# One block of tokens through gathered expert rows, the other three densely, in an expert layer that computes all 16384 experts

## The chip, the core and the metric

The kernel runs on one core of a Trainium2 chip. The metric is the device time of one execution in microseconds (us). The engines of a core run side by side, each through its own queue in order: TensorE (PE in the profile; its weight loads are PEld), VectorE (DVE), ScalarE (ACT), GpSimd (POOL) and SyncE (SP), which issues the transfers (DMA) of the kernel before.

## What is computed

Two transformer blocks in float32 over 512 tokens of width 1024. The first block has two mixing branches and then an expert layer; the second has two layers with a context of 256 tokens and ordinary feed-forward parts. The change lies in the expert layer. There are 128 x 128 = 16384 experts, an input row `peer_u` and an output row `peer_v` of 1024 numbers for each. A token has 8 heads; each head takes the best 16 sums of a first and a second key, so a token has 128 chosen experts with gates:

```python
experts = (i1 * PEER_NKEYS + i2).reshape(t, PEER_HEADS * PEER_TOPK)
gates = jax.nn.softmax(cv, axis=-1).reshape(t, PEER_HEADS * PEER_TOPK)

def token_block(args):
    xb, eb, gb = args
    act = jax.nn.gelu(jnp.einsum('tkd,td->tk', expert_u[eb], xb, preferred_element_type=jnp.float32))
    return jnp.einsum('tk,tkd->td', act * gb, expert_v[eb].astype(jnp.float32)).astype(xb.dtype)
```

The result is added to the residual x, and a norm follows.

## The kernel before

Activations are kept feature-major: x is [128, 8, 512], feature within a tile of 128 on partitions, then the tile, then the token. A product of float32 accuracy is three matmuls in float32r, on a high and a low part of each operand (`mm3`, lines 197 to 199). `wload` brings a block of weights (512 KB), lets ACT copy the high part (line 139, called from there) and DVE subtract the low part (`wl`, line 192).

The expert layer (`peer`) computes every expert for every token, without any gather, in these stages:

- norm and scores: `first_blocks` makes the normed x in two parts (`xh`, `xl`); 16 products with `wq` and the sub-keys give the scores `sc`.
- select (`peer_select`): for each of four tiles of 128 tokens DVE finds the best 16 of each key, the best 16 sums, and their indices; at the end come the gates. The indices and gates are transposed into `iT` (tiles `pi`).
- H (`peer_h`): for each second key j, 24 matmuls over 512 tokens (8 feature tiles times three) give 128 experts' activations, ACT applies gelu, and SP writes them to DRAM (`Hd`). It runs as the filler of the select stage and goes on beside G.
- G (`peer_g`): for each token the two one-hot matrices `oa` and `ob` (DVE, lines 898 and 899), one float32 matmul of them (line 901, two records each) and, for four tokens, one ACT copy to `gs`; SP writes these gates of all experts to DRAM (`Gd`).
- V (`peer_v`): for each j the weights V[j], the activations `pa` and the gates `pg` are loaded, DVE multiplies, ACT and DVE split the product into `ph` and `pl`. Five j form a group; for each of the 8 feature tiles a group takes 15 matmuls into a bank of PSUM, and DVE adds the bank to x.

Then the second block begins with its context part (`ctx0`), beside which `x_entry` norms x.

The order in which instructions are issued is made by `interleave` (line 44): generators ("lanes") yield an assumed time on TensorE and a time until their next piece may start; earlier lanes go first when they are ready, and the filler takes the rest. A half of one j of H counts 2.6 there, a piece of select 0 with a pause of 1.6 to 3.0. PSUM has eight banks: five of tag `bk` (`bank`), two `ac` (`accb`), one `po` (`pob`).

Of the kernel before, what the change touches and what calls it, by code (L numbers as in the profile page):

```python
# [102 lines left out]
class Net:  # L103
# [152 lines left out]
    def rstd(s, pool, T):  # L256
        """1 / rms of every token, from the running sum, on all partitions."""
# [35 lines left out]
    def first_blocks(s, pool, xpool, x, gain, shift, r, aside=None):  # L293
# [1507 lines left out]
```

## Time and profile before

| | us |
|---|---|
| median of 3 runs (lowest to highest) | 4282.54 (4280.67 to 4285.31) |
| the profiled execution, span | 4279.0 |
| busy PE, PEld, DVE, ACT, POOL within the span | 4206.2, 3497.0, 2457.2, 1607.1, 3.5 |
| bytes moved by DMA | 532.83 MB |

The profiled execution has no time of its own beside its span; the median lies 3.5 us above that span. Busy times of PE overlap, since matmuls are pipelined: a matmul's own duration is longer than the step from one start to the next, and it is the step that counts for a stage.

### The profile page before, as it was taken

How to read it: one execution, taken by the hardware profiler on the slowest of the kernel's cores; microseconds unless marked ns; L12 is line 12 of the kernel's file. 1: busy time of each engine (PE TensorE's matmuls, PEld its weight loads, DVE VectorE, ACT ScalarE, POOL GpSimd, SP SyncE). 2: the span in 40 equal slices, each digit the busy share in tenths (PEclk: the TensorE clock that was granted, in tenths of full speed). 3: DMA queues.
4: the chain of work that ended last, by engine and by line, in shares of the span. 5: the costliest groups of instructions: out<-in, count | busy, mean ns of one | idle time of the engine just before them, and what ended most of it. 6: DMA issues, size and time to landing. Idle time of an engine off the chain costs nothing.

```text
span 4279.0 us, 59173 instructions
## 1 busy us (share of the span) xinstructions
PE 4206.2 (98%) x22964; PEld 3497.0 (82%) x22964; DVE 2457.2 (57%) x5635; ACT 1607.1 (38%) x2801; POOL 3.5 (0%) x28
## 2 busy tenths in 40 slices
PE   8999999999999999999999999999999999999998
PEld 5878888887788888888888777888888888887887
DVE  7536554699556665766666665665222256665334
ACT  5335454332233333322222464554211244553222
POOL 0000000000000000000000000000000000000000
PEclk9999999999999999999999999999999999999999
DMA  5341133234445455765666454122112122122232
GB/s 194 106 146 66 45 104 114 78 128 134 152 158 185 168 189 193 240 194 191 191 196 197 170 210 137 35 77 72 60 64 65 62 99 87 45 68 91 94 95 83
DMA packets 219544, 532.83 MB, mean 125 GB/s; under 512 B 24064, under 2 KB 82816, under 8 KB 214784
## 3 DMA queue, kind: packets, MB, share of 16 engines
q1 hardware_dynamic: 219264, 529.06, 37.2%
q8 instruction: 181, 2.97, 0.3%
q14 instruction: 99, 0.81, 0.1%
HBM read 455.58 MB, written 73.40 MB: 124 GB/s over the span
## 4 chain that ended last, share of the span: by engine, by line
PE 88%; DVE 8%; ACT 1%; DMA 1%; issue 1%; SPq 0%; DVEq 0%; ACTq 0%
PE ac L197 21%; PE ac L199 21%; PE ac L198 21%; PE po L401 3%; PE bk L198 3%; PE bk L197 3%; PE bk L199 3%; PE bk L901 3%; PE bk L229 3%; DVE wl L192 1%; PE bk L1017 1%; PE bk L552 1%; PE bk L546 1%; DVE peq L142 1%; DVE psi L814 1%
## 5 line engine op out<-in xcount | busy, mean ns | idle before, releaser
L197 PE MATMUL ac<-xh,wh 128*128 128x512 f32 (+1 forms) x3608 | 1359.3, 378 | 16.0 <-ACT xh L139 7.3
L199 PE MATMUL ac<-xh,wl 128*128 128x512 f32 (+1 forms) x3608 | 1338.7, 372 | 6.1 <-DVE wl L192 5.7
L198 PE MATMUL ac<-xl,wh 128*128 128x512 f32 (+1 forms) x3608 | 1337.8, 372 | 0.9 <-DVE xl L145 0.7
L139 ACT ACTIVATE wh<-wr 128x1024 fp32r<-128x1024 f32 (+1 forms) x599 | 629.5, 1053 | 1723.3 <-PE ac L198 1602.2
L192 DVE TENSOR_TENSOR wl<-wr,wh 128x1024 fp32r<-128x1024 f32 (+1 forms) x599 | 726.5, 1214 | 608.8 <-ACT wh L139 584.7
L197 PEld LDWEIGHTS ac<-xh,wh 128*128 128x128 f32 x3608 | 681.3, 189 | 152.5 <-issue 18.5
L199 PEld LDWEIGHTS ac<-xh,wl 128*128 128x128 f32 x3608 | 680.9, 189 | 137.0 <-DVE wl L192 13.4
L198 PEld LDWEIGHTS ac<-xl,wh 128*128 128x128 f32 x3608 | 681.8, 189 | 121.3 <-issue 7.8
L898 DVE TENSOR_SCALAR oa<-iota,pi 128x128 f32<-128x128 f32 x512 | 144.1, 282 | 148.2 <-PE bk L901 148.2
L197 PE MATMUL bk<-ph,wh 128*128 128x512 f32 x512 | 199.5, 390 | 1.2 <-ACT ph L139 1.2
L198 PE MATMUL bk<-pl,wh 128*128 128x512 f32 x512 | 199.5, 390 | 0.4 <-DVE pl L142 0.4
L199 PE MATMUL bk<-ph,wl 128*128 128x512 f32 x512 | 199.3, 389 | 0.0
L198 PE MATMUL ac<-pl,wh 128*128 128x512 f32 x512 | 199.2, 389 | 0.0
L199 PE MATMUL ac<-ph,wl 128*128 128x512 f32 x512 | 199.2, 389 | 0.0
L197 PE MATMUL ac<-ph,wh 128*128 128x512 f32 x512 | 199.2, 389 | 0.0
L142 DVE TENSOR_TENSOR pa<-pa,pg 128x512 f32<-128x512 f32 x128 | 87.8, 689 | 180.8 <-DMA pg<-Gd 131.0
L198 PE MATMUL ac<-al,wh 128*128 128x512 f32 (+1 forms) x528 | 186.8, 354 | 0.0
L199 PE MATMUL ac<-ah,wl 128*128 128x512 f32 (+1 forms) x528 | 186.8, 354 | 0.0
L197 PE MATMUL ac<-ah,wh 128*128 128x512 f32 (+1 forms) x528 | 186.7, 354 | 0.0
L899 DVE TENSOR_SCALAR ob<-iota,pi,pi 128x128 f32<-128x128 f32 x512 | 174.5, 341 | 0.0
L145 DVE SCALAR_TENSOR_TENSOR x<-ac,mod,x 128x512 f32<-128x512 f32 (+1 forms) x64 | 46.3, 725 | 191.3 <-PE ac L199 191.0
L901 PEld LDWEIGHTS bk<-ob,oa 128*128 128x128 f32 x1024 | 135.1, 191 | 11.3 <-ACT wh L139 0.4
(407 smaller groups left out, 5522.5 us busy)
## 6 DMA issues: line engine op xcount, KB each, us to landing
wr<-win SPq DMA_DIRECT2D x151, 512.0 KB, 3.5
wr<-U SPq DMA_DIRECT2D x128, 512.0 KB, 3.7
wr<-V SPq DMA_DIRECT2D x128, 512.0 KB, 4.6
mw<-wmod SPq DMA_DIRECT2D x96, 512.0 KB, 4.2
Hd<-h SPq DMA_DIRECT2D x128, 256.0 KB, 2.3
pa<-Hd SPq DMA_DIRECT2D x128, 256.0 KB, 4.3
Gd<-gs SPq DMA_DIRECT2D x32, 1024.0 KB, 5.5
pg<-Gd SPq DMA_DIRECT2D x25, 1280.0 KB, 7.9
```

The source lines that it names most:

```text
L139: s.nc.scalar.activation(out, in_, AF.Copy, **kw)
L142: s.nc.vector.tensor_tensor(out, a, b, op=op)
L145: s.nc.vector.scalar_tensor_tensor(out, a, sc, b, op0=op0, op1=op1)
L192: (eng or nc.vector).tensor_tensor(lo[:, :nk, :], raw[:, :nk, :], r32(hi[:, :nk, :]), op=ALU.subtract)
L197: mm(out, ah, bh, start=start, stop=False)
L198: mm(out, ah, bl, start=False, stop=False)
L199: mm(out, al, bh, start=False, stop=stop)
L229: s.nc.tensor.transpose(out, in_, s.ident)
L401: s.nc.tensor.matmul(po, vs[j], pt[:, j, :], start=j == 0, stop=j == nb - 1, skip_group_check=True)
L898: nc.vector.tensor_scalar(a1, iota, iT[0][:, tok:tok + 1], None, op0=ALU.is_equal)
L899: nc.vector.tensor_scalar(a2, iota, iT[1][:, tok:tok + 1], iT[2][:, tok:tok + 1], op0=ALU.is_equal, op1=ALU.mult)
L901: nc.tensor.matmul(b[:, i * 128:(i + 1) * 128], a1, a2, start=True, stop=True)
```

## The change

It leaves the mixing branches and the second block as they are, and does this in the expert layer (TS = 128 tokens, TD = 384):

- The first 128 tokens leave the dense path. Once their choices are known (`rows`, the number of the expert row), `sparse_u` gathers for each of the 128 choices the 128 tokens' rows of `peer_u` (a second copy of that input, laid out in rows, `Ur`): one indirect DMA from GpSimd brings [128 tokens, 1024], 512 KB, into one of six buffers, and DVE multiplies it with the normed x of these tokens (`xt`, token-major, from eight transposes in `first_blocks`) and sums, in one `tensor_tensor_reduce`. Gathers are issued four ahead. Gelu and gates follow.
- `sparse_v` gathers for each of these tokens the 128 rows of `peer_v` (512 KB), four tokens at a time, and sums them with float32 matmuls of 32 columns, one token's weights in one column of a window of zeros, into two banks. Eleven of its 32 steps stand beside G, the rest in V.
- H, G and V handle 384 tokens: the matmuls of H have 384 columns, `Hd` is written for two j at a time, G makes 96 groups of four tokens rather than 128.
- In G the one-hot `oa` is no longer made by DVE: POOL subtracts for four tokens at once, ACT applies Abs and then Relu(1 - a).
- V is turned: the activations are the stationary operand (128 tokens) and V[j] is streamed in two halves of 512 columns; the sums over all 128 j stay in six PSUM banks (three tiles of tokens, two halves), so the adds into x after each group go. At the end eight copies bring the banks to SBUF, 32 transposes and eight adds bring them into x.
- x waits in DRAM (`keep`, 2 MB) from the norm to the end, because four of the six gather buffers lie in its room; SP loads it back when the gathered sums are through.
- The assumed times in the generators change (2.1 for half a j of H, 1.5 rather than 1.7 for G, 4.1 for a j of V).

Comments and docstrings also go; that changes nothing. The diff, cut to its core:

```diff
+TS = 128
+TD = SEQ - TS
...
+                if each:
+                    each(k, t, sl)
...
+                if tt:
+                    s.transpose(b[:, c * 128:(c + 1) * 128], ix)
+                    nc.vector.tensor_copy(iT[c][:, (tt - 1) * 128:tt * 128], b[:, c * 128:(c + 1) * 128])
+            if tt == 0:
+                e = s.t(p, "ppf", [128, 128], 1)
+                s.stt(e, ixs[1], 128.0, ixs[0], ALU.mult, ALU.add)
+                nc.vector.tensor_copy(S["rows"], e)
+                s.transpose(b[:, 0:128], e)
+                nc.vector.tensor_copy(S["rowsT"], b[:, 0:128])
+                S["chosen"] = True
...
+    def gather(s, S, table, idx):
+        g = S["ring"][S["n"] % len(S["ring"])]
+        S["n"] += 1
+        s.nc.gpsimd.indirect_dma_start(out=g, out_offset=None, in_=table,
+                                       in_offset=bass.IndirectOffsetOnAxis(ap=idx, axis=0))
+        return g
+    def sparse_u(s, S):
+        nc = s.nc
+        yield lambda: "chosen" in S
+        act = S["act"]
+        ahead = []
+        for k in range(128 + 4):
+            if k < 128:
+                ahead.append(s.gather(S, s.I["Ur"], S["rows"][:, k:k + 1]))
+            if k >= 4:
+                g = ahead.pop(0)
+                nc.vector.tensor_tensor_reduce(g, g, S["xt"], scale=1.0, scalar=0.0, op0=ALU.mult, op1=ALU.add,
+                                               accum_out=act[:, k - 4:k - 3])
+                yield 0.0, 1.7
+        yield lambda: "gated" in S
+        s.act(act, act, AF.Gelu_apprx_tanh)
+        s.tt(act, act, flat(S["ge"]), ALU.mult)
+        b = s.bank()
+        s.transpose(b[:, 0:128], act)
+        nc.vector.tensor_copy(S["aT"], b[:, 0:128])
+        S["weighted"] = True
+    def sparse_v(s, S):
+        nc = s.nc
+        yield lambda: "weighted" in S
+        rows = s.I["V"].rearrange("j p a b -> (j p) (a b)")
+        po = S["po"] = [s.pob(), s.bank()]
+        aT = S["aT"].rearrange("p (g t) -> p t g", t=32)
+        for t in range(32):
+            gs = [s.gather(S, rows, S["rowsT"][:, 32 * g + t:32 * g + t + 1]) for g in range(4)]
+            w = S["w"][t % len(S["w"])]
+            nc.vector.tensor_copy(w[:, :, 31], aT[:, t, :])
+            for h in range(2):
+                for g in range(4):
+                    nc.tensor.matmul(po[h][32 * g:32 * g + 32, :], w[:, g, 31 - t:63 - t],
+                                     gs[g][:, 512 * h:512 * h + 512], start=t == 0, stop=t == 31,
+                                     skip_group_check=True)
+            yield 2.0, 12.0
+        S["summed"] = True
...
+            ps = s.accb()[:, :TD]
             for k in range(8):
-                s.mm3(ps, w[0][:, k, :], w[1][:, k, :], xh[:, k, :], xl[:, k, :], k == 0, k == 7)
+                s.mm3(ps, w[0][:, k, :], w[1][:, k, :], xh[:, k, TS:], xl[:, k, TS:], k == 0, k == 7)
                 if k == 3:
-                    yield 2.6, 0.0
-            h = s.t(hp, "h", [128, SEQ], 2)
-            s.act(h, ps, AF.Gelu_apprx_tanh)
-            s.nc.sync.dma_start(Hd[j], h)
-            yield 2.6, 0.0
+                    yield 2.1, 0.0
+            if j % 2 == 0:
+                h = s.t(hp, "h", [128, 2, TD], 2)
+            s.act(h[:, j % 2], ps, AF.Gelu_apprx_tanh)
+            if j % 2:
+                s.nc.sync.dma_start(Hd[j // 2], h)
+            yield 2.1, 0.0
...
+        for tb in range(TD // 32):
             gs = s.t(gp, "gs", [128, 128, 32], 2)
             for i4 in range(8):
                 b = s.bank()
+                t0 = tb * 32 + i4 * 4
+                a1 = s.t(gp, "oa", [128, 4, 128], 2)
+                nc.gpsimd.tensor_tensor(a1, iota[:, None, :].to_broadcast([128, 4, 128]),
+                                        iT[0][:, t0:t0 + 4, None].to_broadcast([128, 4, 128]), op=ALU.subtract)
+                nc.scalar.activation(a1, a1, AF.Abs)
+                nc.scalar.activation(a1, a1, AF.Relu, scale=-1.0, bias=1.0)
                 for i in range(4):
-                    tok = tb * 32 + i4 * 4 + i
-                    a1, a2 = s.t(gp, "oa", [128, 128], 4), s.t(gp, "ob", [128, 128], 4)
-                    nc.vector.tensor_scalar(a1, iota, iT[0][:, tok:tok + 1], None, op0=ALU.is_equal)
+                    tok = t0 + i
+                    a2 = s.t(gp, "ob", [128, 128], 4)
                     nc.vector.tensor_scalar(a2, iota, iT[1][:, tok:tok + 1], iT[2][:, tok:tok + 1],
                                             op0=ALU.is_equal, op1=ALU.mult)
-                    nc.tensor.matmul(b[:, i * 128:(i + 1) * 128], a1, a2, start=True, stop=True)
+                    nc.tensor.matmul(b[:, i * 128:(i + 1) * 128], a1[:, i], a2, start=True, stop=True)
                 s.copy(gs[:, :, i4 * 4:i4 * 4 + 4], b.rearrange("p (t i) -> p i t", t=4))
-                yield 0.9, 1.7
+                yield 0.9, 1.5
...
+            Hd = dp.tile([64, 128, 2, TD], F32, name="Hd")
+            Gd = dp.tile([TD // 32, 128, 128, 32], F32, name="Gd")
+            keep = dp.tile([128, 8, SEQ], F32, name="keepx")
...
+                     ring=[flat(x[:, 2 * n:2 * n + 2, :]) for n in range(4)]
+                     + [s.t(sp, f"sr{n}", [128, DM], 1) for n in range(2)])
...
+            su, sv = s.sparse_u(S), s.sparse_v(S)
+            interleave([s.peer_select(p, sc, iota, iT, S), su], hs)
         with ExitStack() as t:
             gp = s.pool(t, "gb")
             s.mark("H+G")
-            interleave([s.peer_g(gp, iota, iT, Gd)], hs)
+            interleave([s.peer_g(gp, iota, iT, Gd), s.until(sv, 12)], hs)
...
+        acc = [[s.accb() if t == 0 else s.bank() for _ in range(2)] for t in range(3)]
+        def dense():
+            js = 0
+            for E in [2] + [6] * 21:
+                g = s.t(p0 if js == 0 else p1, "pg", [128, TD // 32, E, 32], 1 if js == 0 else 2)
+                nc.sync.dma_start(g, Gd[:, :, js:js + E, :].rearrange("b p j t -> p b j t"))
+                for e in range(E):
+                    p, n = (p0, 2) if js % 4 < 2 else (p1, 2)
+                    vh, vl = s.wload(s.I["V"][js], 8, p, n)
+                    if js % 2 == 0:
+                        a = s.t(p0 if js == 0 else p1, "pa", [128, 2, TD], 1 if js == 0 else 2)
+                        nc.sync.dma_start(a, Hd[js // 2])
+                    av = a[:, js % 2].rearrange("p (b t) -> p b t", t=32)
+                    s.tt(av, av, g[:, :, e, :], ALU.mult)
+                    ah, al = s.t(p, "ph", [128, TD], n, F32R), s.t(p, "pl", [128, TD], n, F32R)
+                    s.split(ah, al, a[:, js % 2])
+                    vh, vl = flat(vh), flat(vl)
+                    for h in range(2):
+                        hh = slice(512 * h, 512 * h + 512)
+                        for t in range(3):
+                            tt = slice(128 * t, 128 * t + 128)
+                            s.mm3(acc[t][h], ah[:, tt], al[:, tt], vh[:, hh], vl[:, hh], js == 0, js == 127)
+                    js += 1
+                    yield 4.1, 0.0
+            assert js == 128
+        def reload():
+            yield lambda: "summed" in S
+            for k in range(8):
+                nc.sync.dma_start(x[:, k, :], keep[:, k, :])
+        interleave([sv, reload(), dense()])
+        y = s.t(p1, "py", [128, 4, DM], 1)
+        for h in range(2):
+            hh = slice(512 * h, 512 * h + 512)
+            s.copy(y[:, 0, hh], S["po"][h])
+            for t in range(3):
+                (s.copy if t % 2 else nc.vector.tensor_copy)(y[:, t + 1, hh], acc[t][h])
+        for m in range(8):
+            b = s.bank()
+            for t in range(4):
+                s.transpose(b[:, t * 128:(t + 1) * 128], y[:, t, m * 128:(m + 1) * 128])
+            s.tt(x[:, m, :], x[:, m, :], b, ALU.add)
+            s.squares(p1, x[:, m, :], SEQ)
...
+    A["Ur"] = np.ascontiguousarray(g["peer_u"][0].reshape(128, 128, DM).transpose(1, 0, 2)).reshape(16384, DM)
```

## Rows read from the trace of the kernel before

**Rows 1.** The page: the span and the busy time of each engine.

```profile
span 4279.0 us, 59173 instructions
PE 4206.2 (98%) x22964; PEld 3497.0 (82%) x22964; DVE 2457.2 (57%) x5635; ACT 1607.1 (38%) x2801; POOL 3.5 (0%) x28
```

**Rows 2.** Busy time by stretch: length, then PE, PEld, DVE, ACT, POOL with instruction counts, granted clock, DMA share, GB/s. Select beside H; H beside G; V; the start of the second block.

```profile
885.00:1110.00 225.00, 221.94 (x958) 177.89 (x957) 221.15 (x766) 62.49 (x81) 0.00 (x0) 1.00 0.45 139
1110.00:1697.00 587.00, 587.00 (x3082) 499.90 (x3081) 358.81 (x1151) 209.21 (x310) 0.00 (x0) 1.00 0.49 175
1697.00:2390.00 693.00, 691.39 (x3045) 570.93 (x3044) 433.68 (x584) 210.06 (x261) 0.00 (x0) 1.00 0.62 197
2390.00:2600.00 210.00, 198.85 (x1591) 158.04 (x1591) 143.29 (x361) 114.63 (x267) 0.00 (x0) 0.98 0.59 210
```

**Rows 3.** Timeline of PE where V begins and where it ends: start, duration, instruction; in brackets idle time and what ended it.

```profile
1710.61 0.39 PE L199 MATMUL ac<-xh,wl 128*128 128x512 f32 x1
1710.84 0.39 PE L197 MATMUL bk<-ph,wh 128*128 128x512 f32 x1
...
2410.01 0.39 PE L199 MATMUL ac<-ph,wl 128*128 128x512 f32 x1
2412.62 1.71 PE L260 MATMUL bk<-na,ones 128*128 128x512 f32 x2 [2.23 <-DVE na L142]
```

**Rows 4.** Timeline of PE around 770 us: matmuls of 256 columns before and after a gap.

```profile
768.00 0.28 PE L198 MATMUL bk<-ml,wh 128*128 128x256 f32 x1
768.12 0.28 PE L199 MATMUL bk<-mh,wl 128*128 128x256 f32 x1
...
774.19 0.79 PE L197 MATMUL ac<-xh,wh 128*128 128x256 f32 x2 [3.31 <-ACT xh L139]
...
775.03 0.41 PE L199 MATMUL ac<-xh,wl 128*128 128x256 f32 x1
775.24 0.41 PE L197 MATMUL ac<-xh,wh 128*128 128x256 f32 x1
```

**Rows 5.** Groups of instructions in the stretch 1110 to 1697 us (H beside G): busy us and mean ns of one, idle before and its releaser.

```profile
L899 DVE TENSOR_SCALAR ob<-iota,pi,pi 128x128 f32<-128x128 f32 x512 | 174.5, 341 | 0.0
...
L901 PE MATMUL bk<-ob,oa 128*128 128x128 f32 x1024 | 136.1, 275 | 0.0
...
L192 DVE TENSOR_TENSOR wl<-wr,wh 128x1024 fp32r<-128x1024 f32 x86 | 104.9, 1219 | 64.3 <-ACT wh L139 64.3
L139 ACT ACTIVATE wh<-wr 128x1024 fp32r<-128x1024 f32 x86 | 91.0, 1059 | 201.4 <-PE ac L198 201.4
L139 ACT ACTIVATE gs<-bk 128x512 f32<-128x512 f32 x128 | 76.0, 594 | 177.8 <-PE bk L901 177.8
L133 ACT ACTIVATE h<-ac 128x512 f32<-128x512 f32 x86 | 49.9, 581 | 0.0
```

**Rows 6.** The same stretch 885 to 1110 us as in Rows 2, for line 192 alone: its DVE time and count, clock, DMA.

```profile
885.00:1110.00 225.00, 47.14 (x39) 1.00 0.45 139
```

**Rows 7.** Line 377, the kernel's `tensor_tensor_reduce`, over the whole run: ns min/median/max of one, by form; its read of the sum is a record of its own.

```profile
L377 DVE DVE_READ_ACCUMULATOR2_ANT sv<- x248: 74/83/86, 234.9 to 3841.4; 128x1 f32 x124
L377 DVE CUSTOM_DVE_ANT_0 apr<-bk,b x16: 678/691/693, 234.2 to 575.7; 128x512 f32<-128x512 f32 x16
```

**Rows 8.** Timeline of PE with float32 matmuls of 32 columns in four places of the array (line 1017, 256 columns, four matmuls in eight records): sixteen records and the start of what follows.

```profile
64.05 0.40 PE L198 MATMUL ac<-xl,wh 128*128 128x512 f32 x1
...
72.23 1.07 PE L1017 MATMUL bk<-mw,modl 128*32 128x256 f32 x16
73.24 0.50 PE L197 MATMUL ac<-xh,wh 128*128 128x512 f32 x1
```

**Rows 9.** DMA issues: KB of one, median us from issue to landing; then for V[j] the least, median and longest landing.

```profile
wr<-U SPq DMA_DIRECT2D x128, 512.0 KB, 3.7
wr<-V SPq DMA_DIRECT2D x128, 512.0 KB, 4.6
...
pg<-Gd SPq DMA_DIRECT2D x1, 768.0 KB, 8.2
...
DMA to landing us min/median/max: 3.4/4.6/7.6
```

**Rows 10.** Timeline of SP and of DVE from the last gates to the first product of V.

```profile
1675.95 0.80 SPq L905 DMA_DIRECT2D Gd<-gs  x2
...
1680.18 0.84 SPq L187 DMA_DIRECT2D wr<-U  x1
1681.12 0.83 SPq L975 DMA_DIRECT2D pg<-Gd  x1
...
1691.12 1.28 DVE L142 TENSOR_TENSOR pa<-pa,pg 128x512 f32<-128x512 f32 x2
```

**Rows 11.** Timeline of DVE at the end of V and the start of the second block.

```profile
2410.43 0.69 DVE L142 TENSOR_TENSOR x<-x,ac 128x512 f32<-128x512 f32 x1 [1.26 <-PE ac L199]
2411.88 0.69 DVE L142 TENSOR_TENSOR na<-na,nsq 128x512 f32<-128x512 f32 x1 [0.76 <-ACT nsq L253]
2412.60 0.88 DVE L145 SCALAR_TENSOR_TENSOR nt<-cx,mod,nr 128x256 f32<-128x256 f32 x2
```

**Rows 12.** Busy time of one 50 us stretch at the start of V, columns as in Rows 2.

```profile
1700.00:1750.00 50.00, 48.56 (x211) 38.88 (x210) 34.16 (x42) 22.42 (x26) 0.00 (x0) 1.00 0.78 257
```

More of the change, by code (lines that the diff above doesn't have):

```diff
@@ L291, in last_blocks, with first_blocks @@
         return r
-    def first_blocks(s, pool, xpool, x, gain, shift, r, aside=None):
+    def first_blocks(s, pool, xpool, x, gain, shift, r, aside=None, each=None):
         s.prime(2)
@@ L816, in top16, with peer_select @@
                 nc.vector.match_replace(src, vals[:, 0:8], src, -3.0e38)
-    def peer_select(s, p, sc, iota, iT):
+    def peer_select(s, p, sc, iota, iT, S):
         nc = s.nc
@@ L838, in peer_select @@
             b = s.bank()
+            ixs = []
             for c in range(2):
@@ L846, in peer_select @@
                 ix = s.t(p, "pix", [128, 128], 2)
+                ixs.append(ix)
                 for g in range(2):
@@ L866, in peer_select @@
             s.tt(ge, ge, gm[:, :, None].to_broadcast([128, 8, 16]), ALU.mult)
-            b = s.bank()
-            s.transpose(b[:, 0:128], flat(ge))
-            nc.vector.tensor_copy(iT[2][:, tt * 128:(tt + 1) * 128], b[:, 0:128])
-        for j in range(3):
-            s.dump(f"iT{j}", iT[j])
+            if tt:
+                b = s.bank()
+                s.transpose(b[:, 0:128], flat(ge))
+                nc.vector.tensor_copy(iT[2][:, (tt - 1) * 128:tt * 128], b[:, 0:128])
+        S["gated"] = True
@@ L912, in peer, with peer_hg @@
             dp = s.pool(st, "pd", space=bass.MemoryType.DRAM)
-            Hd = dp.tile([128, 128, SEQ], F32, name="Hd")
-            Gd = dp.tile([16, 128, 128, 32], F32, name="Gd")
+            Hd = dp.tile([64, 128, 2, TD], F32, name="Hd")
+            Gd = dp.tile([TD // 32, 128, 128, 32], F32, name="Gd")
+            keep = dp.tile([128, 8, SEQ], F32, name="keepx")
+            sp = s.pool(st, "sp")
+            S = dict(n=0, rows=s.t(sp, "rows", [128, 128], 1, U32), rowsT=s.t(sp, "rowsT", [128, 128], 1, U32),
+                     ge=s.t(sp, "sge", [128, 8, 16], 1), act=s.t(sp, "sact", [128, 128], 1),
+                     aT=s.t(sp, "saT", [128, 128], 1), xt=s.t(sp, "sxt", [128, DM], 1),
+                     w=[s.t(sp, f"sw{n}", [128, 4, 64], 1) for n in range(3)],
+                     ring=[flat(x[:, 2 * n:2 * n + 2, :]) for n in range(4)]
+                     + [s.t(sp, f"sr{n}", [128, DM], 1) for n in range(2)])
+            for w in S["w"]:
+                nc.gpsimd.memset(w, 0.0)
             v0 = s.pool(st, "pv0")
             with ExitStack() as t:
-                s.peer_hg(t, x, Hd, Gd)
-            s.peer_v(v0, s.pool(st, "pv1"), x, Hd, Gd)
-    def peer_hg(s, st, x, Hd, Gd):
+                sv = s.peer_hg(t, x, Hd, Gd, S, keep)
+            s.peer_v(v0, s.pool(st, "pv1"), x, Hd, Gd, S, sv, keep)
+    def peer_hg(s, st, x, Hd, Gd, S, keep):
         nc = s.nc
@@ L923, in peer_hg @@
         kp = s.pool(st, "pk")
-        iT = [kp.tile([128, SEQ], F32, name=f"pi{j}") for j in range(3)]
+        iT = [kp.tile([128, TD], F32, name=f"pi{j}") for j in range(3)]
         iota = kp.tile([128, 128], F32, name="iota")
@@ L931, in peer_hg, with each @@
         nc.sync.dma_start(gain, s.I["nffn"])
+        box = {}
+        def each(k, t, sl):
+            if sl.start:
+                return
+            if k % 4 == 0:
+                box["b"] = s.bank()
+            s.transpose(box["b"][:, k % 4 * 128:k % 4 * 128 + 128], t[:, 0:TS])
+            if k % 4 == 3:
+                s.copy(S["xt"][:, (k - 3) * 128:(k + 1) * 128], box["b"])
         with ExitStack() as t:
-            (xh, xl), first = s.first_blocks(s.pool(t, "np"), xp, x, gain, None, s.r)
+            (xh, xl), first = s.first_blocks(s.pool(t, "np"), xp, x, gain, None, s.r, each=each)
+            nc.sync.dma_start(keep, x)
         s.mark("scores")
@@ L957, in peer_hg, with until, peer_v @@
             s.mark("H+G")
-            interleave([s.peer_g(gp, iota, iT, Gd)], hs)
+            interleave([s.peer_g(gp, iota, iT, Gd), s.until(sv, 12)], hs)
             for _ in hs:
                 pass
-    def peer_v(s, p0, p1, x, Hd, Gd):
+        return sv
+    @staticmethod
+    def until(gen, n):
+        for _ in range(n):
+            got = next(gen, None)
+            if got is None:
+                return
+            yield got
+    def peer_v(s, p0, p1, x, Hd, Gd, S, sv, keep):
         nc = s.nc
```

34 lines of the change are left out of this document (2 added, 32 removed).

## The prediction

> **What bounds the kernel now.** The busy times first [rows 1]: PE is busy for 98% of the span, so the time is PE's own work unless a stage shows otherwise. Then the stretches of the expert layer [rows 2]: PE is busy throughout, at full granted clock, in select (222 of 225 us), in G (587 of 587) and in V (691 of 693). Next what PE's work costs, which is the step between starts and not a matmul's duration: V's 3072 matmuls of 512 columns run from 1710.8 to 2410.0 [rows 3], less 1.6 us idle [rows 2] 0.227 us each. Of the 3082 records beside G [rows 2] 1024 are G's [rows 5]; the other 2058 at 0.227 are 467, which leaves 120 us, 0.117 each. So H is 3072 x 0.227 = 697 us, G 120, V 699. Last, who is next: DVE in select, busy 221 of 225 us [rows 2], but ahead of PE, which does not wait for it.
>
> **What is removed.** H keeps its number of matmuls and goes from 512 to 384 columns. Matmuls of 256 columns follow each other every 0.12 us [rows 4] with the same weight loads of 128 x 128, so a step goes with columns; 384 lies midway, (0.12 + 0.227) / 2 = 0.1735. H becomes 533 us (-164). G falls to 96 groups: 768 records x 0.117 = 90 (-30). V falls from 24 to 18 matmuls per j at 512 columns: 2304 x 0.227 = 523 (-176). The adds into x after each group of V also go, worth nothing: DVE has 434 busy us of 693 there [rows 2].
>
> **What PE gets.** The gathered rows of `peer_v` are summed by eight float32 matmuls of 32 columns and 512 streamed per step. The same form with 256 streamed takes 1.01 us for eight [rows 8], so 2.0 for 512: 32 steps are 64 us, 22 beside G and 42 in V. The eight transposes at the norm are 1 us.
>
> **DVE in select becomes the bound.** From 885 us on select has 221 - 47 = 174 us of DVE work left [rows 2, 6]; what it did before then, beside the scores, stays there. New are 128 sums over 1024 columns. A `tensor_tensor_reduce` of 512 takes 0.691 plus 0.083 for the read of the sum [rows 7]; a two-input operation of 1024 takes 1.219 [rows 5]; so 1.30 each, 167 us. To this come the `wl` of each j that H issues meanwhile. How many is plain from the issue rule: the filler H goes in halves of j, now 2.1, before 2.6. A pause of 2.4 or 2.6 was covered by one half and now needs two. Per tile of tokens: 16 pieces x 2 halves + 4 x (1 + 2) = 44 halves, 22 j; four tiles and the gates make 90 j where it was 58. DVE: 174 + 167 + 90 x 1.22 = 451 us from 885 to 1336. PE: 90 x 24 x 0.1735 = 375 us from 894 (1710.8 - 697 - 120) to 1269. PE idles about 66 us, in the second half of the stage: the first tile's choices come early, and up to j = 48 DVE keeps up. Bounds: 0, if DVE's sums fall where PE has work in hand; 100, if each sum took a third more.
>
> **The gathers.** No row shows an indirect DMA or any transfer issued by POOL. The nearest is V[j], the same 512 KB in 128 rows of 4 KB from SP: 3.4 to 7.6 us from issue to landing, median 4.6 [rows 9]. With four in flight that is one every 1.2 to 1.9 us, one at a time one every 4.6, at worst 7.6; at the rate that the DMA reaches in V (197 GB/s at a share of 0.62, so 318 when full [rows 2]) 1.65. A sum needs one every 3.5 us (451 / 128), a step of `sparse_v` four per 14 us. I take them as hidden, nearest to the case in flight. DMA as a whole: select then moves 128 x 0.52 + 90 x (0.52 + 0.20) MB = 132 MB in 451 us, 293 GB/s; its rate at full share now is 139 / 0.45 = 309 [rows 2]. Weights will land late at times; 10 us, between 0 and 40.
>
> **G.** 38 j are left for 96 groups, half a j per group, so H ends at about group 76 to 89, and PE works 4 x 2 x 0.117 + 12 x 0.1735 = 3.0 us per group. ACT per group: the copy 0.59, Abs and Relu at about 0.6 each (the 512-column forms there are 0.58 to 0.59), half a j's 1.06 + 0.5 [rows 5]: 2.6. DVE: 4 x 0.34 + 0.6. POOL's subtraction is shown by no row; between one token's `ob` on DVE, 0.34, and four of them, 1.36 [rows 5]; I take 1.4. All fit under 3.0, barely for ACT, so I put 20 us here: the last groups without H go at ACT's 1.8 instead of 0.94, and the two `oa` buffers hold one group's chain (1.4 + 0.6 + 0.6 and queueing) against the next. Bounds 0 and 58 (3.6 us per group).
> The profile shows no operation of POOL beside two-input ones of DVE. [...]
>
> **Entry of V.** The last gates are issued at 1675.95, their reload at 1681.1, the first product comes at 1691.1, all under H's last j [rows 10]. [...] 12 us.
>
> **V.** A step of `sparse_v` comes with three j: PE 2.0 + 3 x 4.09 = 14.3 us. DMA: 4 x 0.52 for rows, per j 0.52 + 0.20 + 0.20, together 4.85 MB, at 318 GB/s 15.3 us. So PE is short of data by 1 us per step, 21 us, and 4 for x's reload: 25, between 0 and 97 (at 257 GB/s, the rate of the stretch in which V starts [rows 12]). V: 523 + 42 + 25 = 590.
>
> **The tail.** Before, 2.6 us after V's last matmul the norm's matmul runs [rows 3]. Now copies (1.3), then eight adds and eight sums of squares on DVE at 0.69 each [rows 11], 11 us, and DVE is busy without a gap behind it: +10.
>
> **The sum.** Before: 697 + 120 + 699 = 1516. After: 533 + 90 + 22 + 66 + 10 + 20 + 12 = 753, 590, 10: 1353. -163 from the span of 4279.0, plus 3.5 to the median: 4120.
>
> **The rivals.**
> 1. PE stays the bound throughout: sums, one-hots and gathers all hide (no 66, 10, 20, 25). 4000. For it: PE has never waited for DVE in select so far. Against: DVE has 4 us of 225 to spare there and gets 167 more.
> 2. More is lost than I put: V's gathers at 257 GB/s (+72) and G at 3.6 us a group (+38). 4230 with both, 4180 to 4250.
> 3. Slower: the gathers are the pace, POOL issuing one after another. With c us each, select ends at 905 + 128 c, G and the entry of V take 302 after that, V 21 x 4 c + 65 x 4.09: V's end is 1483 + 212 c against 2410. It decides from c = 4.4. At V[j]'s median of 4.6, one at a time, 4331; at 7.6, 4967. For it: nothing shows what an indirect DMA costs POOL. Against: four may be in flight, and SP's own issue is short. [...]
> 4. The work does not shrink as it should: 384 columns cost as much as 512, because weight loads set the step. H stays at 697, the DVE wait vanishes under it: about 4220. The steps of 0.12 at 256 columns [rows 4] speak against it.
>
> **Chances.** The forecast (4060 to 4180) 0.53; rival 1 (3980 to 4060) 0.13; rival 2 and 4 (4180 to 4270) 0.18; rival 3 0.13; within 0.2% 0.03. The range 3980 to 4240 holds 0.8 of this: all but rival 3, the 0.03 and the worst of rival 2. 0.2% (8.6 us) is about what a measurement of this kernel can tell from no change; faster 0.84, same 0.03, slower 0.13.
>
> **What would show it.** Right: PE's idle time in select before `wl`, about 66 us, DVE full to about 1340; steps of 0.17 in H and 0.227 in V; V starting near 1645 and lasting 590. Wrong: DVE idle before the sums with a gather as releaser (rival 3); PE without gaps in select (rival 1); V's idle time behind `wr`, `pg` or gathered rows far above 25 us, or steps above 3.0 us a group in G (rival 2); H at 0.227 a step (rival 4).

## The result, and the profile after

The kernel after the change takes 4103.65 us (median of 4 runs, 4098.85 to 4120.5), beside 4281.6 us of the kernel before (4 runs, 4280.39 to 4285.31). The ratio is 0.959, 95% interval 0.9573 to 0.9606: 178 us faster, where 4120 had been forecast. The profiled execution has a span of 4099.0 us, 180.0 less than before [rows 1].

The page of the kernel after, its first lines and the queue of the gathers:

```profile
span 4099.0 us, 58251 instructions
PE 3947.8 (96%) x22491; PEld 3315.5 (81%) x22491; DVE 2378.3 (58%) x5089; ACT 1682.5 (41%) x2968; POOL 387.6 (9%) x383
...
q0 software_dynamic: 36864, 134.23, 8.8%
```

PE lost 258 busy us and gained idle time: 98% became 96%. q0 is new: these are the gathers, 256 x 512 KB.

Busy time by stretch, columns as in [rows 2]: most of select, G with H beside it, the end of G up to V's first dense matmul, V up to its last sparse step, the rest of V; then two pieces of select.

```profile
930.00:1330.00 400.00, 355.58 (x1954) 346.22 (x1953) 395.41 (x1010) 125.61 (x175) 149.11 (x129) 0.95 0.84 319
1330.00:1580.00 250.00, 246.75 (x1670) 225.18 (x1669) 199.14 (x380) 189.70 (x318) 132.38 (x127) 1.00 0.77 277
1580.00:1646.00 66.00, 48.83 (x229) 25.70 (x228) 31.68 (x61) 28.69 (x48) 31.39 (x31) 0.90 0.76 272
1646.00:1935.00 289.00, 284.25 (x1337) 211.21 (x1338) 127.00 (x195) 92.13 (x123) 62.67 (x58) 0.99 0.85 303
1935.00:2221.00 286.00, 280.77 (x1227) 229.11 (x1228) 142.56 (x203) 103.14 (x134) 0.00 (x0) 1.00 0.64 218
...
1180.00:1230.00 50.00, 31.12 (x135) 28.35 (x134) 50.00 (x162) 8.62 (x12) 13.55 (x11) 0.80 0.57 189
1280.00:1330.00 50.00, 36.45 (x193) 34.41 (x192) 47.44 (x112) 20.30 (x29) 8.60 (x9) 0.83 0.60 222
```

In select PE idles 44 of 400 us and DVE is full; before, both were full [rows 2]. Of the 44 us, 32 lie in the two pieces of the last rows: there DVE is busy for 97 of 100 us, and the DMA for less than two thirds of the time. G runs nearly without loss, the 66 us ahead of V do not, and V idles 10 us.

Timeline of PE of the kernel after, in six places (answers to [rows 3] and [rows 4]):

```profile
1194.81 0.34 PE L201 MATMUL ac<-xl,wh 128*128 128x384 f32 x1
1194.98 0.34 PE L202 MATMUL ac<-xh,wl 128*128 128x384 f32 x1
1196.67 0.45 PE L200 MATMUL ac<-xh,wh 128*128 128x384 f32 x1 [1.35 <-ACT h L136]
...
1199.37 0.33 PE L232 MATMUL bk<-ident,pix 128*128 128x128 f32 x1 [2.08 <-DVE pix L862]
1202.56 0.69 PE L202 MATMUL ac<-xh,wl 128*128 128x384 f32 x1 [2.86 <-DVE wl L195]
1203.04 0.52 PE L200 MATMUL ac<-xh,wh 128*128 128x384 f32 x1
1203.36 0.52 PE L201 MATMUL ac<-xl,wh 128*128 128x384 f32 x1
...
1636.01 1.36 PE L933 MATMUL po<-sr,sw 128*32 128x512 f32 x2 [3.77 <-DMA sr<-V,rowsT]
...
1646.08 0.80 PE L200 MATMUL ac<-wh,ph 128*128 128x512 f32 x1 [5.23 <-ACT ph L142]
...
2220.48 0.39 PE L202 MATMUL bk<-wh,pl 128*128 128x512 f32 x1
2220.71 3.65 PE L232 MATMUL bk<-ident,py 128*128 128x128 f32 x32
2231.13 2.05 PE L263 MATMUL bk<-na,ones 128*128 128x512 f32 x2 [6.76 <-DVE na L145]
```

Three things are to be seen. H's steps of 384 columns are 0.17 us apart. After a row of waits (1.35, 2.08 and 2.86 us) they are 0.32 apart for a while, at a granted clock of 0.50 (1203.0 to 1206.4). And V runs from 1646.08 to 2220.71, 574.6 us, with 10.4 us from there to the norm's matmul (2.6 before [rows 3]).

What PE waited for in select, and what DVE did there: groups of instructions from 930 to 1330 us, of PE and then of DVE, the idle time before them behind the second bar.

```profile
L200 PE MATMUL ac<-xh,wh 128*128 128x384 f32 x646 | 223.0, 345 | 24.6 <-ACT h L136 24.6
L202 PE MATMUL ac<-xh,wl 128*128 128x384 f32 x646 | 220.7, 342 | 4.0 <-DVE wl L195 4.0
L232 PE MATMUL bk<-ident,pix 128*128 128x128 f32 x6 | 2.4, 408 | 15.5 <-DVE pix L862 15.5
...
L908 DVE CUSTOM_DVE_ANT_0 x<-x,sxt 128x1024 f32<-128x1024 f32 x84 | 101.9, 1214 | 0.0
L195 DVE TENSOR_TENSOR wl<-wr,wh 128x1024 fp32r<-128x1024 f32 x83 | 101.8, 1226 | 4.2 <-ACT wh L142 4.2
L908 DVE CUSTOM_DVE_ANT_0 sr<-sr,sxt 128x1024 f32<-128x1024 f32 x42 | 50.9, 1214 | 0.4 <-DMA sr<-Ur,rows 0.4
```

DVE hardly waits for gathered rows here (0.4 us). The 24.6 us on the gelu `h` name ScalarE, which is itself idle two thirds of the stage: 76 of the 81 gelus there start 0.96 to 0.97 us after the start of the `wh` issued ahead of them, and what stood ahead was late. For 7.0 us of them that was a piece of the gates, which had waited 10.8 us for DVE; for 6.9 us `wh`, whose block of weights had not landed; for 8.9 us `wh` again, which went on after work of DVE, or of PE, which had itself been waiting for `wl`. A block of U is asked for only when `wl` has freed its buffer (`wl` done at 956.72, the next block issued at 956.75), so a late `wl` and a slow landing add up. The DMA of the same stretch, its busy tenths and GB/s in 40 slices of 10 us, and its issues:

```profile
DMA  9999999999999544689999999434968999999512
GB/s 409 407 315 317 395 416 415 414 411 412 412 416 401 161 145 152 201 272 380 415 393 398 368 394 380 158 105 158 327 195 336 379 362 414 411 381 386 201 52 92
...
wr<-U SPq DMA_DIRECT2D x83, 512.0 KB, 6.8
...
x<-Ur,rows POOLq DMA_INDIRECT x81, 8.8
```

It comes in bursts: up to 416 GB/s for 100 us at a time, and under 200 between them. A U block takes 6.8 us to land, where it took 3.7 [rows 9]. So two things are full in select, though not at the same times, and the profile alone does not say what PE would gain if one of them were eased.

### The profile page after: what moved, and what is told of

Read it like the earlier page. It is cut to its first block, busy times and chain, and to the rows that moved or that the text cites. A ratio compares the mean times of both kernels' runs of the same rounds, so it can differ in the third digit from the quotient of the medians.

```text
span 4099.0 us, 58251 instructions
## 1 busy us (share of the span) xinstructions
PE 3947.8 (96%) x22491; PEld 3315.5 (81%) x22491; DVE 2378.3 (58%) x5089; ACT 1682.5 (41%) x2968; POOL 387.6 (9%) x383
## 4 chain that ended last, share of the span: by engine, by line
PE 54%; DVE 6%; DMA 6%; issue 1%; ACT 1%; POOL 0%; DVEq 0%; SPq 0%; ACTq 0%; POOLq 0%
PE ac L200 13%; PE ac L201 13%; PE ac L202 13%; DMA pa<-Hd 5%; PE po L406 3%; PE bk L975 2%; DVE wl L195 2%; PE bk L232 2%; PE bk L201 1%; PE bk L200 1%; PE bk L202 1%; DVE pl L145 1%; PE po L933 1%; PE bk L1301 1%; PE bk L1145 1%
## 5 line engine op out<-in xcount | busy, mean ns | idle before, releaser
L200 PE MATMUL ac<-xh,wh 128*128 128x512 f32 (+2 forms) x3608 | 1302.5, 362 | 38.2 <-ACT h L136 24.6
L202 PE MATMUL ac<-xh,wl 128*128 128x512 f32 (+2 forms) x3608 | 1282.0, 356 | 7.0 <-DVE wl L195 7.0
L201 PE MATMUL ac<-xl,wh 128*128 128x512 f32 (+2 forms) x3608 | 1283.1, 356 | 1.0 <-DVE xl L148 0.7
L145 DVE TENSOR_TENSOR pa<-pa,pg 128x384 f32<-128x384 f32 x128 | 66.3, 555 | 293.0 <-DMA pa<-Hd 281.6
L201 PE MATMUL bk<-wl,ph 128*128 128x512 f32 x512 | 200.4, 391 | 0.0
L200 PE MATMUL bk<-wh,ph 128*128 128x512 f32 x512 | 200.4, 391 | 0.0
L202 PE MATMUL bk<-wh,pl 128*128 128x512 f32 x512 | 200.2, 391 | 0.0
L142 ACT ACTIVATE ph<-pa 128x384 fp32r<-128x384 f32 x128 | 66.9, 523 | 185.7 <-PE bk L201 84.8
L892 POOL DMA_INDIRECT x<-Ur,rows x86 | 101.0, 1175 | 347.7 <-DVE psv L818 205.4
L975 PEld LDWEIGHTS bk<-ob,oa 128*128 128x128 f32 x768 | 98.4, 191 | 24.6 <-ACT oa L969 7.7
L966 POOL TENSOR_TENSOR oa<-iota,pi 128x512 f32<-128x512 f32 x96 | 101.9, 1062 | 150.6 <-PE bk L975 117.9
```

Source lines behind the costliest of these rows:

```text
L142: s.nc.scalar.activation(out, in_, AF.Copy, **kw)
L145: s.nc.vector.tensor_tensor(out, a, b, op=op)
L200: mm(out, ah, bh, start=start, stop=False)
L201: mm(out, ah, bl, start=False, stop=False)
L202: mm(out, al, bh, start=False, stop=stop)
L892: s.nc.gpsimd.indirect_dma_start(out=g, out_offset=None, in_=table, in_offset=bass.IndirectOffsetOnAxis(ap=idx, axis=0))
```

## The experiments

Theory A is the prediction's: VectorE's sums are what TensorE waits for in select. Its rival B: the gathers load the DMA, weights come late, and the full VectorE is only beside it. All times below are medians of 4 or 5 runs, each beside runs of the kernel before; "change" is against 4103.65, whose own runs lie 22 us apart, so that less than some 10 us says little.

**Half of each sum.**

```diff
-tensor_tensor_reduce(g, g, S["xt"], ...)
+tensor_tensor_reduce(g[:, 0:512], g[:, 0:512], S["xt"][:, 0:512], ...)
```

> Each of the 128 sums of the sparse part takes only the first 512 of the 1024 columns (half of each dot product is left out); the gathers stay whole. Theory A (VectorE's sums are what TensorE waits for in select): a sum falls from 1.28 us to about 0.77, VectorE gets 65 us less, TensorE's idle time of some 45 us in select nearly goes, time -30 to -45 us. Theory B (the gathers load the DMA so that weights land late, and VectorE's fullness is only beside it): no change within 8 us.

4093.39 us (ratio 0.9549, 0.9533 to 0.9565): change -10. A missed by 20 us at least; B's limit of 8 is passed by 2, which the runs can't tell. Groups of DVE, then of PE, 930 to 1330 us, of this kernel:

```profile
L908 DVE CUSTOM_DVE_ANT_0 x<-x,sxt 128x512 f32<-128x512 f32 x85 | 58.0, 686 | 15.8 <-DMA x<-Ur,rows 15.5
L908 DVE CUSTOM_DVE_ANT_0 sr<-sr,sxt 128x512 f32<-128x512 f32 x42 | 28.7, 686 | 13.4 <-DMA sr<-Ur,rows 13.3
...
L202 PE MATMUL ac<-xh,wl 128*128 128x384 f32 x653 | 224.8, 344 | 30.3 <-DVE wl L195 30.0
```

The sums did get 66 us cheaper, and now DVE waits 29 us for gathered rows; `wl`, behind them in DVE's queue, is late, and PE still idles 36 us, 30 of them for it. From 1180 to 1230 us the DMA's share is now 1.01, where it was 0.57. No run issued the U gathers more than four ahead, so that their number may have a part in this as well as the DMA's rate.

**Half of the U gathers.**

```diff
-ahead.append(s.gather(S, s.I["Ur"], S["rows"][:, k:k + 1]))
+ahead.append(s.gather(...) if k % 2 == 0 else ahead[-1])
```

> Every second of the 128 gathers of U rows is left out; its sum is taken over the rows gathered before, so VectorE does all 128 sums (every second dot product is wrong). Theory A (VectorE is the bound): less than 10 us change. Theory B (DMA is the bound): 33 MB less in select, 20 to 45 us faster, and the landing of weights for U falls from 6.5 us towards 3.7.

4104.58 us (0.9586, 0.957 to 0.9602): change +1. The DMA fell to 237 GB/s in the stretch, DVE stayed full (396.6 of 400), PE idle 39 us. This is what A had said, and B falls: as the kernel stands, the DMA is not what PE pays for.

**Both at once.** The two edits together.

> Half of each sum's columns and every second U gather are left out at once (the dot products are wrong). With the sums alone halved the time fell by only some 10 us, since the DMA then ran at 412 GB/s and VectorE waited 29 us for gathered rows; with the gathers alone halved it did not fall. Theory C (two bounds of nearly equal height in select, VectorE and DMA, either of which holds TensorE): both together give more than the sum of the two, -35 to -45 us, and TensorE loses less than 12 us between 930 and 1330. Rival (the choice of experts itself, its chains and its order, makes most of the idle time): -10 to -15 us, as with the sums alone.

4063.43 us (0.9486, 0.947 to 0.9502): change -40, where the two alone make -9 between them. Busy time from 930 to 1330 us of this kernel:

```profile
930.00:1330.00 400.00, 392.35 (x2258) 372.11 (x2260) 366.14 (x1082) 158.35 (x232) 101.75 (x94) 1.00 0.78 267
```

PE idles 8 us in place of 44 and its clock is whole. This settles select: two bounds of nearly equal height, DVE first and the gathers, with the DMA in its bursts, close behind it; either holds PE when the other is eased.

**No sparse part.** Sums, gathers and their products are left out; `y[:, 0]` is set to zero.

```diff
-interleave([s.peer_select(p, sc, iota, iT, S), su], hs)
+interleave([s.peer_select(p, sc, iota, iT, S)], hs)
...
-interleave([s.peer_g(gp, iota, iT, Gd), s.until(sv, 12)], hs)
+interleave([s.peer_g(gp, iota, iT, Gd)], hs)
...
-interleave([sv, reload(), dense()])
+interleave([reload(), dense()])
```

> The whole sparse part is left out (no gathers, no sums, no products with gathered rows; the first 128 tokens get no experts). It prices that part. Theory A: 45 us of idle TensorE in select, 64 us of its matmuls and some 5 us of waits in V go: 3980 to 4000 us. Theory B (the DMA load of the gathers costs everywhere): more, 3930 to 3970. If the idle time of select comes from the choice of experts itself, not from the sums: 4020 to 4040.

3975.18 us (0.9282, 0.9266 to 0.9297), 5 below A's range and 5 above B's: the sparse part costs 128 us. Select, G and V of this kernel:

```profile
930.00:1330.00 400.00, 392.93 (x2274) 384.06 (x2273) 296.60 (x808) 163.88 (x240) 20.80 (x19) 1.00 0.53 173
1330.00:1567.00 237.00, 209.55 (x1334) 205.48 (x1333) 175.70 (x350) 180.64 (x299) 81.02 (x77) 0.93 0.55 194
1567.00:2093.00 526.00, 524.94 (x2305) 433.37 (x2305) 269.88 (x381) 190.21 (x252) 0.00 (x0) 1.00 0.65 219
```

The choice of experts by itself holds PE for 7 of 400 us only. V is 526 us, 3 above its 2304 steps of 0.227; with the sparse steps it was 574.6. The idle 27 us in the second row are the open entry of V, which the sparse steps fill in part in the full kernel.

**512 columns in H.** It undoes the removed columns alone.

```diff
-ps = s.accb()[:, :TD]
+pf = s.accb()
+ps = pf[:, TS:]
...
-s.mm3(ps, ..., xh[:, k, TS:], xl[:, k, TS:], k == 0, k == 7)
+s.mm3(pf, ..., xh[:, k, :], xl[:, k, :], k == 0, k == 7)
```

> H is computed for all 512 tokens again, as before the change (128 columns too many, not used); all else as after it. It prices the removed columns. Steps go back from 0.174 to 0.227 us, 3072 of them: 164 us more work of TensorE. If VectorE and DMA hold TensorE back in select (theory C), the longer steps hide part or all of the 45 us idle there: 4103.65 + 164 - (25 to 45) = 4223 to 4243 us. If the idle time is a matter of the order alone and stays: 4260 to 4270.

4211.62 us (0.9829, 0.9812 to 0.9845): 108 more, not 164, and below the range of either. The same three stretches:

```profile
930.00:1330.00 400.00, 395.82 (x1702) 316.14 (x1702) 377.30 (x964) 102.14 (x142) 153.04 (x126) 1.00 0.81 299
1330.00:1759.00 429.00, 411.44 (x2218) 321.51 (x2217) 250.50 (x479) 255.98 (x403) 189.64 (x160) 0.99 0.64 225
1759.00:2336.00 577.00, 565.75 (x2565) 440.58 (x2566) 270.07 (x396) 194.53 (x255) 67.75 (x58) 0.99 0.74 260
```

PE is without gaps in select again (4 us idle, full clock), and V starts 113 us later: 51 us of the 164 are hidden under work that was waiting in the kernel after. That is more than the 44 idle us, since the steps at the lower clock go too (the granted clock in the first stretch is 1.00, in the kernel after 0.95). So of the 164 us that H saves, about a third is not received.

**32 sums moved beside G.** The helper `then` runs one generator after the other.

```diff
-interleave([s.peer_select(p, sc, iota, iT, S), su], hs)
+interleave([s.peer_select(p, sc, iota, iT, S), s.until(su, 97)], hs)
...
-interleave([s.peer_g(gp, iota, iT, Gd), s.until(sv, 12)], hs)
+interleave([s.peer_g(gp, iota, iT, Gd), s.then(su, s.until(sv, 12))], hs)
```

> The last 32 of the 128 sums (with their gathers) are issued beside G in place of select; nothing is left out. Theory A: 41 us of VectorE work leave the stage where it is the bound, and H keeps more matmuls for G; -20 to -40 us. Theory B: no change within 8 us. Rival C (VectorE is then late in G as well): the gain in select is given back, -10 to +15, with TensorE's idle time in G behind the one-hots of VectorE.

4107.82 us (0.9588, 0.9572 to 0.9604): change +4, a miss for A, within the ranges of both B and C. It tells little: about as many sums as before were done by 1230 us, PE's loss of 17 us from 1180 to 1230 stayed, and the moved sums ran from 1230 on, where DVE was full too.

**48 sums moved, the others spaced.** As above with 81 for 97, and:

```diff
-                yield 0.0, 1.7
+                yield 0.0, 3.8 if k % 2 else 1.7
```

> 80 of the 128 sums are issued beside select, every second one with a longer pause behind it (so that H gets two half steps there), the other 48 beside G; nothing is left out. In the run with 32 sums moved, 97 sums were still done by 1230 us, as many as before, so that it did not test the crowded stretch. Theory A or C: fewer sums and gathers before 1230, TensorE's loss there (17 to 19 us at 1180 to 1230) goes, -15 to -35 us. Rival (VectorE has no more room in G than in select): within 10 us of the kernel after the change, the idle time only moves.

4132.06 us (0.9641, 0.9625 to 0.9657): change +28, a miss, and outside what the rival named. V of this kernel:

```profile
1638.00:2261.00 623.00, 603.71 (x2683) 447.94 (x2683) 271.39 (x404) 195.04 (x255) 96.29 (x87) 0.99 0.76 266
```

V begins 8 us earlier only, and lasts 623 us: the products with V rows could start at 1537 us instead of 1330, so 23 of the 32 steps (372 of 512 matmuls) fell into V, and V is 55 us above 523 and 23 x 1.94, where it was 21 above with 16 steps. Each of these steps costs V 2.3 us beyond its matmuls, where it was 1.3.

**A quarter of the V gathers.** Matmuls unchanged.

```diff
-gs = [s.gather(S, rows, S["rowsT"][:, 32 * g + t:32 * g + t + 1]) for g in range(4)]
+gs = [s.gather(S, rows, S["rowsT"][:, t:t + 1])] * 4
```

> In the product with gathered rows of V, one gather in place of four per step serves all four groups (wrong rows for three of four); matmuls unchanged. 50 MB less, two thirds of it beside V and the end of G. If the DMA load of these gathers holds V back (forecast: 25 us; V took 574.6 us, 523 of it dense matmuls and 31 these): V falls by 8 to 18 us and the entry of V (waits of 5.4 and 3.8 us for gathered rows) by up to 9 more: -10 to -25 us. If not: within 5 us, V's remaining excess is from elsewhere.

4060.4 us (0.9475, 0.9459 to 0.9491): change -43; the profiled spans differ by 36. The end of G and V of this kernel:

```profile
1580.00:1637.00 57.00, 48.35 (x350) 28.50 (x348) 32.19 (x69) 30.53 (x49) 24.03 (x23) 0.98 0.77 264
1637.00:2185.00 548.00, 545.71 (x2455) 436.79 (x2456) 273.62 (x391) 191.78 (x256) 4.38 (x4) 1.00 0.66 220
```

V holds 150 sparse matmuls (9.4 steps): 523 + 18 + 7. Its excess falls from 21 to 7; 3 us of it were there without a sparse part, so a step's share falls from 1.1 to 0.4 us, and the rest of the fall is that 6.6 steps fewer lie in V. V begins 9 us earlier although these 6.6 steps (13 us) went ahead of it. So with the gathers go most of the excess in V and some 22 us ahead of it, more than expected. A quarter of the gathers also frees buffers sooner and makes a step wait for one landing in place of four; the run does not part this from the load on the DMA.

**The one-hot on DVE.** A comparison in place of GpSimd's subtraction and two passes of ScalarE.

```diff
-nc.gpsimd.tensor_tensor(a1, iota..., iT[0]..., op=ALU.subtract)
-nc.scalar.activation(a1, a1, AF.Abs)
-nc.scalar.activation(a1, a1, AF.Relu, scale=-1.0, bias=1.0)
+s.tt(a1, iota..., iT[0]..., ALU.is_equal)
```

> The first one-hot factor of G is made by one comparison on VectorE for four tokens, in place of a subtraction on GpSimd and two passes of ScalarE; same result. If the tensor_scalar on VectorE (mean 528 ns beside GpSimd, 341 before) is stretched by GpSimd's subtraction, it falls back to 345 ns, VectorE's work in G stays about level (60 us more, 70 us less), ScalarE loses 121 us, GpSimd's 30 us pause at 1296 goes: -5 to -20 us. Rival (VectorE then is the bound in G, the stretch has another cause): +5 to +30 us.

4093.85 us (0.9558, 0.9542 to 0.9574): change -10. Groups of DVE from 1326 to 1646 us, first of the kernel after, then of this one:

```profile
L973 DVE TENSOR_SCALAR ob<-iota,pi,pi 128x128 f32<-128x128 f32 x384 | 177.7, 528 | 58.5 <-PE bk L975 58.2
L195 DVE TENSOR_TENSOR wl<-wr,wh 128x1024 fp32r<-128x1024 f32 x42 | 58.5, 1394 | 14.6 <-ACT wh L142 14.4
```

```profile
L971 DVE TENSOR_SCALAR ob<-iota,pi,pi 128x128 f32<-128x128 f32 x384 | 109.4, 349 | 64.6 <-PE bk L973 61.1
L145 DVE TENSOR_TENSOR oa<-iota,pi 128x512 f32<-128x512 f32 x96 | 65.7, 684 | 0.0
L195 DVE TENSOR_TENSOR wl<-wr,wh 128x1024 fp32r<-128x1024 f32 x43 | 52.2, 1218 | 0.7 <-ACT wh L142 0.5 <-issue 0.2
```

With GpSimd's 96 subtractions `ob` was 68 us longer and `wl` 6 us: the work that GpSimd took from DVE (66 us) it took back from it. The run also drops ScalarE's two passes, but the trace of the kernel after tells the two apart: of its 84 `ob` above 0.45 us, 81 overlap a subtraction (159 overlap one, mean 0.79 us), and the 225 that overlap none took 0.34 on average; one that began at 1399.48, with a subtraction running from 1399.49 to 1400.53, took 1.13. `wl` shows the same: from 1326 to 1646 us 1.68 in the 16 that overlap a subtraction, 1.22 in the 25 others. Why the two take longer there, no run shows.

**GpSimd's arithmetic used early.**

```diff
+nc.gpsimd.tensor_tensor(flat(S["w"][2]), flat(S["w"][0]), flat(S["w"][1]), op=ALU.subtract)
```

> One small subtraction on GpSimd is added ahead of select, before any gather. If GpSimd's pause of 30 us ahead of its first subtraction is paid once (the first use of that kind of operation), it moves out of the way and the idle TensorE around 1300 to 1340 shrinks: -3 to -12 us. If it is paid at each change from gathers to arithmetic, the pause at about 1296 stays and the time doesn't change.

4107.31 us (0.9585, 0.9569 to 0.9601): no change. Timeline of POOL in this run, then of PE and POOL in the kernel after:

```profile
1329.12 2.03 POOL L966 TENSOR_TENSOR oa<-iota,pi 128x512 f32<-128x512 f32 x2 [31.57 <-issue]
...
1325.47 0.41 PE L232 MATMUL bk<-ident,pge 128*128 128x128 f32 x1
1326.03 2.04 POOL L966 TENSOR_TENSOR oa<-iota,pi 128x512 f32<-128x512 f32 x2 [30.16 <-issue]
```

The pause of some 31 us before the first subtraction after the gathers came again, so it isn't a matter of first use. Nor is it one of a change from gathers to arithmetic: GpSimd waits for the end of select. The first subtraction starts 0.14 to 0.15 us after PE has transposed the last gates (`pge`): at 1326.03 after 1325.88 in the kernel after, at 1329.12 after 1328.98 here, and at the same distance in eight other runs, one of them without any gather. Its length follows from that: 0.3 us with 48 sums moved, 74 with both halves, 125 with 512 columns in H. It costs nothing by itself: in the run without subtractions PE lost as much from 1280 to 1330 (15.4 us idle, in the kernel after 13.6).

**Sparse steps of V spaced.** On top of the one-hot on DVE:

```diff
-            yield 2.0, 12.0
+            yield 2.0, 12.0 if t < 12 else 22.0
```

> Two edits, both with the full result: the one-hot on VectorE (alone: 4093.85 us), and the sparse steps beside V spaced over the whole stage (pause 22 instead of 12 from the 13th step on), so that the DMA carries their gathers at an even rate in place of a share of 0.86 in V's first half and 0.64 in its second. If crowding of the DMA in V's first half costs time: 5 to 12 us below the one-hot alone, 4082 to 4089 us. If V waits for no crowding: 4090 to 4098.

4077.08 us (0.9522, 0.9506 to 0.9538): change -27, 17 below the one-hot alone, better than expected. V takes 566 us with 16 steps, 12 above 523 and 31.5, where with the one-hot alone it took 582; the DMA's share is 0.77 in its first half (1628 to 1911) and 0.75 in its second, where it was 0.84 and 0.64.

**Sums spaced too.** On top of that, all sums beside select:

```diff
-                yield 0.0, 1.7
+                yield 0.0, 1.7 if k % 3 else 3.8
```

> The last kernel (one-hot on VectorE, sparse steps beside V spaced; 4077.08 us) and one more edit, the full result kept: all 128 sums stay beside select, but every third one has a pause of 3.8 in place of 1.7 behind it, so that H gets two half steps there and the sums and gathers come less densely. Theory C: TensorE loses less of its 45 us in select (25 to 35), H keeps fewer matmuls for G, where VectorE is freer since the one-hots: 4055 to 4072 us. Rival (as in the run that spread the sums into G, what is won in select is lost in G, which now has fewer matmuls of H beside it): 4073 to 4100 us.

4077.81 us (0.9524, 0.9511 to 0.9537): the rival was right. Select and G of the kernel before this edit, then of this one:

```profile
930.00:1330.00 400.00, 355.05 (x1954) 347.13 (x1953) 393.84 (x1008) 123.32 (x171) 145.97 (x128) 0.95 0.84 319
1330.00:1630.00 300.00, 288.57 (x1903) 251.22 (x1903) 213.33 (x540) 111.79 (x176) 68.59 (x63) 0.99 0.80 290
```

```profile
930.00:1330.00 400.00, 375.69 (x2098) 366.78 (x2097) 393.28 (x999) 131.49 (x182) 140.54 (x123) 0.97 0.85 318
1330.00:1630.00 300.00, 276.60 (x1782) 230.76 (x1782) 212.15 (x549) 105.14 (x166) 84.78 (x73) 0.99 0.81 294
```

PE wins 20.6 us in select and loses 12.0 in G, the rest later: H's matmuls are the filler of both stages and there are only 3072 of them. These two are the best versions found that leave nothing out, 27 and 26 us below the change.

## Why the prediction was right, point by point

**H, G, V by columns: right.** A step of 384 columns is 0.174 us (forecast 0.1735), the steps of V stayed at 0.227, and V without the sparse part is 526 (523). Rival 4 falls.

**Select: right in cause, too dear by 17 us, and blind to the next bound.** Forecast: 66 us of idle time for DVE and 10 for late weights. Measured from 930 to 1330: 44.4 us idle and, beyond that, 14.4 us of slow steps. The second number: 1938 matmuls of H in the stretch at 0.174 are 337 us, the others with the transposes about 4, but PE was busy 355.6. Together 59. DVE was full as forecast, a sum with its read cost 1.21 + 0.08 (1.30), H had done 91 j by 1326 us (90 by 1336), and with the gathers halved nothing came back. What the forecast missed is how close the gathers stand behind DVE: with the sums halved only 10 us came back. It took the mean, 293 GB/s of a full 309, and put 10 us beside DVE's 66. The rate was wrong: the DMA reached 416 GB/s. And the mean hides the bursts: the DMA was busy for 9 tenths or more in 27 of the 40 slices and for under 6 tenths in 9 others. Two more slips changed little: the bound of 100 for sums a third dearer would be 122 (66 + 167 / 3), and PE had waited for DVE in select before (2.7 us for `wl`, 885 to 1110 us), not never.

**G and the entry of V: sum right, places wrong.** Forecast 20 and 12. From 1330 to 1580 PE lost 3 us, so `oa`'s chain did not hold it. From 1580 to 1646 PE's work is 48 x 0.174 + 101 x 0.117 + 5 sparse steps x 1.94 = 30 us, which leaves 36 of 66: 17 idle, the rest in steps that took longer (the granted clock was 0.90), not taken apart further. H was used up at 1592, as foreseen; but what then filled the gap, the sparse steps, waited for their rows (5.4, 3.8 us), and the last 5.2 us are the reload's. No run shows the 12 us of the entry as one term; what the runs showed in its place are these three waits, 14.4 us. With a quarter of the V gathers the part ahead of V shrinks by some 22 us.

**What the forecast had no term for:** the longer times of DVE's instructions beside GpSimd's subtraction. The profile before had little to price them from: its memsets on GpSimd met a DVE operation on two tensors only at 41.1 us. `ob` was costed at 0.34 us and took 0.53 on average, 0.79 beside a subtraction. It had little price in G, where PE lost 3 us, and 10 us by the run without it, which spares ScalarE work too.

**V: 590 forecast, 574.6 measured.** Sixteen sparse steps fell into it, not 21 (31 us in place of 42), at 1.94 us each (2.0); the excess is 21 (25). Of this, 3 remain without the sparse part; the other 18 are 1.1 us a step (1 in the forecast), and with a quarter of the gathers 0.4. The term was right in size, and most of it goes with the gathers, as it said.

**Tail:** +7.8 (10.4 less 2.6), forecast +10.

**The sum.** From 894, where the forecast starts to count, to 1646.08 are 752 us (H begins at some 884 in both kernels; about 9 us of other work are left out of both sums): H 535, G 90, sparse steps 31, select 59, the end of G 39, less 2 of rounding; forecast 753. The gain of 180 against 163 in the forecast is nearly all V's 15. The total for the stages ahead of V came out to 1 us partly by luck: the sparse steps beside G were 9 us longer than put, select 17 cheaper, the entry dearer.

**The rivals.** 1 (PE the bound throughout, 4000) would need both bounds of select gone; with both eased, and G and V left as they are, it is 4063. 2 falls by G's 3 us and V's 21. 3, the slower one, decided from 4.4 us per gather (its 1483 is 10 more than its terms, which does not move the 4.4): a gather holds POOL for 0.94 us (median), and four in flight land at a median of 7.9 us under load, 4.1 at the least. Line 892 of the kernel after:

```profile
L892 POOL DMA_INDIRECT x<-Ur,rows x86: 937/939/2007, 919.2 to 1281.1; - x86
...
DMA to landing us min/median/max: 4.1/7.9/12.5
```

DVE waited 4.3 us for them in all.

## What to carry to other kernels

Where a stage gets two new loads at once (here sums on VectorE and gathers on the DMA), ease each alone and both together before you name the bound: -10, +1 and -40 us say that VectorE is the first and the gathers the next. A saving on the engine that bounds is received only up to the next bound: of 164 us saved in H about two thirds arrived, and in select long waits cost again in the slower steps behind them (0.32 us in place of 0.174 after a wait of 3.82). Filler work is a fixed stock: taking more of it for one stage empties the next, so spread the loads (the V gathers, -17 us) before moving the filler.

## What the runs showed of the hardware

- After a row of waits of 1.35, 2.08 and 2.86 us, TensorE's steps of 384 columns were 0.32 us apart in place of 0.174, from 1203.0 to 1206.4 us of the kernel after, at a granted clock of 0.50; after one wait of 3.82 us, which ended at 1218.06, again (0.50 from 1218.5 to 1223). Behind one wait of 1.35 us, which ended at 1209.81, they were 0.17 apart from the second on (granted clock 1.00). From 1180 to 1230 us the granted clock was 0.80 on average. In select the slower steps cost some 14 us (an estimate from the busy time beyond the steps) beside 44 us idle.
- The DMA moved up to 416 GB/s (10 us of select in the kernel after) with gathers and weights in flight together; from 930 to 1330 us a 512 KB block from SP took 6.8 us to land and a gather of 128 rows of 4 KB 8.8 (medians).
- A gather of 128 rows occupied GpSimd for 0.94 us in the kernel after (median; 0.93 to 2.01).
- A `tensor_scalar` of 128 x 128 on VectorE (`ob` of the kernel after), 0.34 us where it overlapped no subtraction of GpSimd, took 0.79 on average and up to 1.83 in the 159 that overlapped one. Beside a gather alone it took 0.35.
